# Sparse attention in two groups of four heads, the first woven with a convolution tile and query projections, and a rotation done by transfers

## The chip, the cores and the metric

The kernel runs on one core of one Trainium2 chip. The metric is device time in microseconds (us): the median of three runs, and beside it one execution that was profiled. TensorE (PE) multiplies, VectorE (DVE) and ScalarE (ACT) work on rows of up to 128 partitions, GpSimd (POOL) does small powers and issues some transfers, SyncE (SP) issues most transfers. Transfers may also be issued from the ACT queue.

## The reference

Two layers in float32 on 512 positions of width 1024. The change touches the mixing step of the second layer, where eight heads of a sparse attention stand beside a causal convolution:

```python
def partial_rope(x, cos, sin):                 # the first 16 of each 64 channels are rotated
    x1, x2 = xr[..., :8], xr[..., 8:16]
    rot = jnp.concatenate([x1 * cos - x2 * sin, x2 * cos + x1 * sin], axis=-1)
    return jnp.concatenate([rot.astype(x.dtype), x[..., 16:]], axis=-1)

def dsa_attention(q, k, v, qi, ki, wi):        # for each block of 128 queries
    rel = jax.nn.relu(jnp.einsum('bqhd,bsd->bqhs', qib, ki))
    score = jnp.einsum('bqh,bqhs->bqs', wib, rel)           # index scores, 4 heads
    _, sel = lax.top_k(where(causal, score, -inf), 128)     # 128 keys are kept for each query
    logits = einsum(qb, k[sel]) * (64 ** -0.5)              # 8 heads, one key and value head
    p = softmax(where(sel <= t, logits, -inf)); return einsum(p, v[sel])

q, k, v, qi, ki, wi, glu = jnp.split(rmsnorm(x) @ w_in, cuts, axis=-1)
u = causal_dwconv(ga * sigmoid(gg), conv_b_w, conv_b_b)     # 31 taps, 512 channels
b_out = jax.nn.silu(layernorm(u))
x = x + jnp.concatenate([a_out, b_out], axis=-1) @ w_out
```

## The kernel before

Activations lie transposed (channels on partitions, 512 positions along the free dimension), in pairs of a rounded part (hi) and a remainder (lo). A projection is eight times three matmuls (lines 385 to 387: hi*hi, lo*hi, hi*lo) of 128 channels by 512 positions, so 24 for one output tile. Its weights come by an SP transfer into `raw`, are cast to `whi` on ACT (L361), and the remainder `wlo` is taken on DVE in two halves (L364).

`mix_2` is the stage that changes. It has these parts, in this order:

- `sparse_in` turns the projections `qi` (two tiles) and `ki` into rotated tiles by `roped_2`, and computes the index scores (L1518, six matmuls for a pair of heads and a block of queries), ReLU on ACT (L1486) and the weighted sum `acc` on DVE (L1489, L1491).
- `top_rounds` finds the mask: for each of the query blocks 1, 2 and 3, sixteen rounds of a MAX8 (L1575) and a MATCH_REPLACE8 (L1576) over 256, 384 or 512 keys, all on DVE, each round on the result of the one ahead of it. L1578 ends a block and makes `acc` an additive mask. This chain is woven (`jobs.weave`) with a queue of jobs that mostly need PE: the four pairs of convolution inputs (`conv_in`, 48 matmuls each), three convolution tiles (`conv`, L1695), the key and value projection (`sparse_kv`), the query projections (`sparse_q`, two times 48), and the last convolution tile.
- `sparse_attend` does the attention in 16 steps (a block of queries, a pair of heads): `scores` (six matmuls L1518, on DVE the mask and the row maximum L1604, on ACT the exponential L1606), one step later `turn` (transposes L1616, copied to SBUF L1618), one step later `values` (L1629). At the last pair of a block the sums are inverted, turned (L1638) and multiplied in. It is woven with `conv_out` (layer norm of the convolution), whose transposes are L1732 and L1747. PE runs this part in the order in which the code is written (`manual_schedule`); everywhere else a scheduler orders the instructions of each engine.

`roped_2` rotates one tile. It copies the projection to `x` on ACT (L1527), swaps rows 0 to 7 with rows 8 to 15 of each 64 by a matmul with a constant permutation (L1529), forms x*C2 (L1530), swapped*S2 (L1532) and their sum (L1533) on DVE, and splits the sum in hi on ACT (L409) and lo on DVE (L410). Rows 16 and up have S2 = 0. It is called eight times: twice for `qi`, once for `ki`, once for the key, four times for the queries. `x` and the result `t` come from a ring `t2` of three buffers that also holds `rel`, `dex` and `don`. For `ki` and the key, `both_halves` then copies 64 rows onto the other 64 by two SP transfers (L1510).

The first layer has a similar swap by transfers already (`swap`, L1501: transfers of 32 rows, issued on the ACT queue).

Of the kernel before, what the change touches and what calls it, by code (L numbers as in the profile page):

```python
# [30 lines left out]
NT = 4  # L31
# [8 lines left out]
def _constants():  # L40
# [17 lines left out]
    put("perm2", (i == np.where(m < 8, p + 8, np.where(m < 16, p - 8, -1))[None, :]))  # L58
# [175 lines left out]
FILL = 32  # L234


class Builder:
# [1283 lines left out]
    def roped_2(self, p, dst, ps, n, rows=None):  # L1521
# [58 lines left out]
    def sparse_attend(self, p, tbs, acc, qT, kv, mix):  # L1580
# [5 lines left out]
        R = [p.tile([128, 4, 540], F32, name="ds", tag="R", bufs=2), p.tile([128, 4, 512], F32, name="dPT")]  # L1586
        ring = lambda k, n: R[k][:, n % 4, :512]
        turns = [0, 0]

        def slot(k):  # L1590
            turns[k] += 1
            return ring(k, turns[k])

        def scores(tb, h0):
            n = (tb + 1) * 128
            msk = acc[tb][:, :n] if tb else self.c("swm")[:, 128:256]
            if h0 == 0:
                S["st", tb] = p.tile([128, 4, 8], F32, name="dst", tag="dst", bufs=2)
            st = S["st", tb]
            pss = [self.psum(t) for t in ("at", "mm")]  # L1600
            self.scores_pair(pss, qT[h0 // 2], kT, tb)
            for h, ps in zip((h0, h0 + 1), pss):
                s = S[tb, h] = slot(0)
# [4 lines left out]
            return 0.00334 * n  # L1608

        def turn(tb, h0):  # L1610
            n = (tb + 1) * 128
            for h in (h0, h0 + 1):
                pt = self.psum("rw")
                s = S.pop((tb, h))
                for c in range(tb + 1):
                    tr(pt[:, c * 128:(c + 1) * 128], s[:, c * 128:(c + 1) * 128], self.ident)  # L1616
                PT = S["PT", tb, h] = slot(1)
                (V.tensor_copy if h % 2 else nc.scalar.copy)(PT[:, :n], pt[:, :n])  # L1618
            return 0.22 * (tb + 1)

        def values(tb, h0):

            if h0 == 0:
                S["po"] = self.psum("po")
            po, st, j = S["po"], S["st", tb], h0 // 2
# [5 lines left out]
            if h0 < 6:  # L1631
                return 0.42 * (tb + 1)
            V.reciprocal(st[:, 3], st[:, 2])
            ex = p.tile([128, 512], F32, name="dex", tag="t2", bufs=self.t2n)
# [329 lines left out]
```

## Time and profile before

| | |
|---|---|
| median of three runs | 1451.52 us (1449.52 to 1459.29) |
| profiled execution, its own time | 1450.54 us |
| its span | 1448.8 us |
| PE busy, mean granted clock | 97% of the span, 0.988 |
| DVE, ACT, POOL busy | 60%, 39%, 6% |
| `mix_2` with the end of the norm ahead of it, 728 to 909.8 us | 181.8 us, granted clock 0.94 |

A row of the stretches gives the time of each stretch, the time in which each engine worked in it, and the granted clock of TensorE (1.00 is 2.4 GHz, 0.50 is 1.2 GHz). Idle time of an engine counts where another engine waits for it.

### The profile page before, as it was taken

The page shows a single profiled execution, that of the slowest core. Times are in us where ns is not written, and L with a number is a line of the kernel's source. Part 1 is how long each engine was busy: PE and PEld are TensorE (multiplying, and loading weights), DVE is VectorE, ACT ScalarE, POOL GpSimd, SP SyncE. Part 2 cuts the span into 40 slices and gives each one's busy share as a digit, 9 for nine tenths or more (in the row PEclk, how much of TensorE's full clock was granted, in tenths as well). Part 3 has the DMA queues.
Part 4 walks back from the last instruction along what each step waited for, and adds up shares of the span by engine and source line. Part 5 has one row for each costly group of instructions (what it writes and reads, how often), then busy time and mean ns, then how long its engine had stood idle before and what let it go on. Part 6 is the DMA issues. An engine that isn't in the chain of part 4 may idle for free.

```text
span 1448.8 us, 20320 instructions
## 1 busy us (share of the span) xinstructions
PE 1407.9 (97%) x7876; PEld 1113.7 (77%) x7876; DVE 870.5 (60%) x1983; ACT 557.9 (39%) x964; POOL 89.7 (6%) x164
## 2 busy tenths in 40 slices
PE   8799999999999999999999999999999999999998
PEld 6688768876776887887867556888888888888886
DVE  4768567776756775347569957465465555554232
ACT  4534345444344322333432126443344334343122
POOL 1101011201001000000001100000000000000000
PEclk9999999999999999999999998999999999999999
DMA  8367314422222441325226510252122332332221
GB/s 277 119 187 224 106 39 122 122 61 81 74 73 67 138 131 60 123 69 187 66 66 158 133 59 1 74 190 87 59 88 88 106 99 88 105 99 102 102 87 73
DMA packets 143617, 151.65 MB, mean 105 GB/s; under 512 B 22305, under 2 KB 118945, under 8 KB 143009
## 3 DMA queue, kind: packets, MB, share of 16 engines
q1 hardware_dynamic: 129088, 124.93, 27.6%
q0 software_dynamic: 4480, 14.98, 3.8%
q10 hardware_dynamic: 9952, 10.45, 2.2%
q8 instruction: 62, 1.02, 0.3%
q14 instruction: 35, 0.28, 0.1%
HBM read 135.33 MB, written 13.18 MB: 103 GB/s over the span
## 4 chain that ended last, share of the span: by engine, by line
PE 77%; DVE 8%; issue 2%; ACT 1%; POOL 1%; DMA 1%; ACTq 0%; POOLq 0%; DVEq 0%; SPq 0%
PE ps_mm L385 17%; PE ps_mm L386 17%; PE ps_mm L387 16%; DVE acc L1576 2%; PE ps_at L385 2%; PE ps_rw L385 2%; PE ps_at L387 2%; PE ps_at L386 2%; PE ps_rw L387 2%; PE ps_rw L386 2%; DVE m L1575 2%; DVE wlo L364 1%; PE ps_po L643 1%; PE ps_at L1518 1%; PE ps_at L614 1%
## 5 line engine op out<-in xcount | busy, mean ns | idle before, releaser
L364 DVE TENSOR_TENSOR wlo<-raw,whi 128x512 fp32r<-128x512 f32 x412 | 272.7, 683 | 279.4 <-ACT whi L361 276.1
L361 ACT CAST whi<-raw 128x1024 fp32r<-128x1024 f32 (+1 forms) x206 | 215.9, 1049 | 454.1 <-PE ps_mm L386 247.6
L386 PE MATMUL ps_mm<-blo,whi 128*128 128x512 f32 (+2 forms) x544 | 208.9, 384 | 0.0
L385 PE MATMUL ps_mm<-bhi,whi 128*128 128x512 f32 (+2 forms) x544 | 208.3, 383 | 0.0
L387 PE MATMUL ps_mm<-bhi,wlo 128*128 128x512 f32 (+2 forms) x544 | 207.6, 382 | 0.0
L385 PE MATMUL ps_mm<-hhi,whi 128*128 128x512 f32 (+1 forms) x488 | 195.2, 400 | 0.2 <-ACT hhi L409 0.2
L386 PE MATMUL ps_mm<-hlo,whi 128*128 128x512 f32 (+1 forms) x488 | 192.4, 394 | 0.8 <-DVE hlo L410 0.8
L387 PE MATMUL ps_mm<-hhi,wlo 128*128 128x512 f32 (+1 forms) x488 | 192.4, 394 | 0.0
L386 PEld LDWEIGHTS ps_mm<-blo,whi 128*128 128x128 f32 (+1 forms) x544 | 102.1, 188 | 22.9 <-issue 3.3
L385 PEld LDWEIGHTS ps_mm<-bhi,whi 128*128 128x128 f32 (+1 forms) x544 | 102.0, 188 | 21.5 <-issue 1.8
L387 PEld LDWEIGHTS ps_mm<-bhi,wlo 128*128 128x128 f32 (+1 forms) x544 | 102.0, 188 | 21.4 <-issue 1.8
L385 PEld LDWEIGHTS ps_mm<-hhi,whi 128*128 128x128 f32 x488 | 92.7, 190 | 20.4 <-issue 3.4
L387 PEld LDWEIGHTS ps_mm<-hhi,wlo 128*128 128x128 f32 x488 | 92.8, 190 | 18.2 <-issue 1.8
L386 PEld LDWEIGHTS ps_mm<-hlo,whi 128*128 128x128 f32 x488 | 92.7, 190 | 17.7 <-DVE hlo L410 1.3
L995 DVE TENSOR_TENSOR tmp<-U,L 32x31 f32<-32x31 f32 (+30 forms) x124 | 37.9, 306 | 4.2 <-DMA L<-lspill 2.0
L385 PE MATMUL ps_mm<-yhi,whi 128*128 128x512 f32 x96 | 39.1, 409 | 0.5 <-DVE ga L1183 0.3
L997 DVE TENSOR_TENSOR U<-U,tmp 32x31 f32<-32x31 f32 (+30 forms) x124 | 38.0, 306 | 2.3
L386 PE MATMUL ps_mm<-ylo,whi 128*128 128x512 f32 x96 | 38.7, 404 | 0.0
L387 PE MATMUL ps_mm<-yhi,wlo 128*128 128x512 f32 x96 | 38.3, 399 | 0.0
L421 ACT ACTIVATE nxs<-x 128x1024 f32<-128x1024 f32 x16 | 17.0, 1060 | 32.3 <-DVE x L1210 28.7
L1695 PE MATMUL ps_yk<-R,diag 128*32 128x512 f32 x256 | 29.3, 594 | 0.0
L385 PE MATMUL ps_mm<-mT,whi 128*128 128x256 f32 x96 | 28.0, 291 | 0.7 <-DVE kvt L410 0.6
(478 smaller groups left out, 2629.4 us busy)
## 6 DMA issues: line engine op xcount, KB each, us to landing
raw<-in_w_in_dram SPq DMA_DIRECT2D x24, 1024.0 KB, 5.3
raw<-in_w_in_dram SPq DMA_DIRECT2D x26, 512.0 KB, 3.9
raw<-in_w_gate_dram SPq DMA_DIRECT2D x11, 1024.0 KB, 5.1
raw<-in_w_up_dram SPq DMA_DIRECT2D x11, 1024.0 KB, 5.1
raw<-in_w_down_dram SPq DMA_DIRECT2D x10, 1024.0 KB, 4.9
raw<-in_w_out_dram SPq DMA_DIRECT2D x8, 1024.0 KB, 4.9
R<-cspill POOLq DMA_DIRECT2D x16, 270.0 KB, 6.0
raw<-in_w_k_cross_dram SPq DMA_DIRECT2D x4, 1024.0 KB, 7.8
```

What stands on the lines that cost most here:

```text
L361: nc.scalar.copy(h, v)
L364: self.last_lo = nc.vector.tensor_tensor(l[:, x], v[:, x], h[:, x].bitcast(F32), op=OP.subtract)
L385: mm(ps, L[0], R[0], start=first, stop=False)
L386: mm(ps, L[0], R[1], start=False, stop=False)
L387: mm(ps, L[1], R[0], start=False, stop=last)
L421: nc.scalar.activation(sc, x, AF.Square, accum_out=ss[:, 0:1])
L614: mm(pv[r][:, :n], q[64 * r:64 * r + 64, tb * 128:(tb + 1) * 128], kT[64 * r:64 * r + 64, key0:key0 + n], start=True, stop=True)
L995: V.tensor_tensor(t, U32[:np_, 0:a, m:m + 1].to_broadcast([np_, a, w]), L32[m // 16][:np_, m % 16:m % 16 + 1, m + 1:32].to_broadcast([np_, ...
L997: V.tensor_tensor(U32[:np_, 0:a, m + 1:32], U32[:np_, 0:a, m + 1:32], t, op=OP.add)
L1575: V.max(m, acc[tb][:, :n])
L1576: V.match_replace(acc[tb][:, :n], m, acc[tb][:, :n], DEAD)
L1695: nc.tensor.matmul(ps[32 * b:32 * b + 32], diag(i)[:, b * 8 + g, :], R[:, b, 4 * g:4 * g + 512], start=g == 0, stop=g == 7)
```

## The change

The rotation: the matmul with the permutation goes. Instead the rows of `x` are moved to `t` by transfers on the ACT queue, three for each 64 rows (8 rows, 8 rows, and 48 rows that are copied in place so that `t` is defined), so six for a tile of 128 rows. The product with S2 is then taken in place from `t`. A constant column block goes, and a filler in SBUF grows by as much, which keeps addresses.

The attention: it runs as two groups `g` of four heads. Within a group the blocks of queries are paired as (0, 3) and (1, 2), and steps alternate between the two blocks of a pair; one normalisation serves both blocks of a pair. Group 0 uses two buffers "at" for its scores and is woven with the last convolution tile and the second pair of query projections. Group 1 uses "at" and "mm" and has nothing written between its steps. `conv_out` follows it in the code and is left to the scheduler.

```diff
@@ roped_2
         nc.scalar.copy(x[:rows], ps[:rows])
-        pp = self.psum("at")
-        nc.tensor.matmul(pp[:n], self.c("perm2")[:n, :n], x[:n], start=True, stop=True)
+        t = p.tile([128, 512], F32, name="ry2", tag="t2", bufs=self.t2n)
+        for h in range(0, n, 64):
+            for d, r, k in ((0, 8, 8), (8, 0, 8), (16, 16, 48)):
+                nc.scalar.dma_start(t[h + d:h + d + k], x[h + r:h + r + k])
+        V.tensor_tensor(t[:n], t[:n], S2[:n], op=OP.mult)
         V.tensor_tensor(x[:n], x[:n], C2[:n], op=OP.mult)
-        t = p.tile([128, 512], F32, name="ry2", tag="t2", bufs=self.t2n)
-        V.tensor_tensor(t[:n], pp[:n], S2[:n], op=OP.mult)
         V.tensor_tensor(t[:n], x[:n], t[:n], op=OP.add)
@@ sparse_attend
-        steps = [(tb, h) for tb in tbs for h in range(0, 8, 2)]
-        for i in range(len(steps) + 2):
+        steps = [(G, i, h0) for G in ((0, 3), (1, 2)) for h0 in (0, 2) for i in range(2)]
+        for n in range(len(steps) + 2):
             for k, f in enumerate((scores, turn, values)):
-                if 0 <= i - k < len(steps):
-                    yield f(*steps[i - k])
+                if 0 <= n - k < len(steps):
+                    f(*steps[n - k])
+            yield fill
@@ mix_2
-        jobs.add(ci[0], dj[0], ci[1], dj[1], co[0], dj[2], ci[2], co[1], dj[3], ci[3], co[2], self.sparse_kv(p, hT, kv),
-                 self.sparse_q(p, hT, 0, qT), co[3], self.sparse_q(p, hT, 1, qT))
+        jobs.add(ci[0], dj[0], ci[1], dj[1], co[0], dj[2], ci[2], co[1], dj[3], ci[3],
+                 self.sparse_kv(p, hT, kv), self.sparse_q(p, hT, 0, qT), co[2])
         jobs.weave(self.top_rounds(p, acc), self.SC2[0])
+        jobs.run(lambda: not jobs.q)
+        tail = Jobs()
+        tail.add(co[3], self.sparse_q(p, hT, 1, qT))
+        tail.load(tail.q[1])
         jobs.run()
+        jobs = tail
         mix = self.act_tiles("h")
-        jobs.add((None, lambda _: self.sparse_attend(p, range(NT), acc, qT, kv, mix)))
+        self.rings, self.turns = [], [0, 0]
+        attend = lambda g, tags, fill: self.sparse_attend(p, g, acc, qT, kv, mix, tags, fill)
         with self.tc.manual_schedule(engines={mybir.EngineType.PE}):
-            jobs.weave(self.conv_out(p, cv, mix), self.SC2[1])
+            jobs.weave(attend(0, ("at", "at"), 1.0), self.SC2[1])
             jobs.run()
+            for _ in attend(1, ("at", "mm"), 0.0):
+                pass
+        for _ in self.conv_out(p, cv, mix):
+            pass
         return mix
-    SC2 = (1.3, 18.0)
+    SC2 = (1.3, 1.9)
```

Three places show the new order. The first is ACT at the rotations of `sparse_in` (`rx` is x, `ry` is t, `hl` a rotated tile). Before:

```order
L1527 COPY rx_6584<-ps_mm 128x512
L361 CAST whi<-raw 128x1024
L1527 COPY rx_6596<-ps_mm 128x512
L409 CAST hl<-ry_6589 128x512
L409 CAST hl<-ry_6601 128x512
L361 CAST whi<-raw 128x1024
L1527 COPY rx_6640<-ps_mm 68x512
L409 CAST hl<-ry_6645 64x512
```

and now, with the lines of the changed kernel:

```order
L1526 COPY rx_6600<-ps_mm 128x512
L360 CAST whi<-raw 128x1024 x2
L408 CAST hl<-ry_6586 128x512
L1530 DMA ry_6602<-rx_6600 8x512 x2
L1530 DMA ry_6602<-rx_6600 48x512
L1530 DMA ry_6602<-rx_6600 8x512 x2
L1530 DMA ry_6602<-rx_6600 48x512
L1526 COPY rx_6648<-ps_mm 68x512
L360 CAST whi<-raw 128x1024
L1679 ACTIVATE sth<-ps_mm 128x512
L408 CAST hl<-ry_6602 128x512
L1530 DMA ry_6650<-rx_6648 8x512 x2
```

The transfers of the second tile stand behind the cast of the first rotated tile, and those of `ki` behind the cast of the second.

The second is DVE at the end of the rounds. Before, L1578 of block 3 stands right behind the last round and all of the key's and queries' rotation behind it:

```order
L1575 MAX m_7275<-acc 128x8
L1576 MATCH_REPLACE acc<-m_7275,acc 128x512
L1578 TENSOR_SCALAR acc<-acc 128x512
L1530 TENSOR_TENSOR rx_7348<-rx_7348,rp_6109 64x512
L1532 TENSOR_TENSOR ry_7353<-ps_at,rp_6109 64x512
```

Now the rotations of the key and of one query tile stand among the rounds, and of the next query tile its first product does:

```order
L1575 MAX m_7295<-acc 128x8
L1576 MATCH_REPLACE acc<-m_7295,acc 128x512
L1531 TENSOR_TENSOR ry_7412<-ry_7412,rp_6109 128x512
L1578 TENSOR_SCALAR acc<-acc 128x512
L1532 TENSOR_TENSOR rx_7410<-rx_7410,rp_6109 128x512
L1608 ISA ds,dst<-ps_at,acc 128x512
```

The third is PE where the attention begins (`ps_yk<-R,diag` is the convolution). Before, after the last rotation:

```order
L1732 MATMUL ps_yk<-cst,cv 128x128 x4
L1529 MATMUL ps_at<-rx_7551,cst 128x512
L1518 MATMUL ps_at<-hl 128x256
L1518 MATMUL ps_mm<-hl 128x256
L1518 MATMUL ps_at<-hl 128x256
```

and now:

```order
L1703 MATMUL ps_yk<-R,diag 32x512 x32
L1517 MATMUL ps_at<-hl 128x256 x6
L1703 MATMUL ps_yk<-R,diag 32x512 x12
L1517 MATMUL ps_at<-hl 128x512 x6
L1620 MATMUL ps_rw<-cst,ds 128x128 x2
L1703 MATMUL ps_yk<-R,diag 32x512 x8
L1517 MATMUL ps_at<-hl 128x256 x6
```

Blocks 0 and 3 now come first, with pieces of the last convolution tile between them. From the first rotation to the first index score PE has 24 projection matmuls for `ki` and then 20 others before, 79 others now; from the last index score to the first attention score it has 166 projection matmuls and three convolution tiles now. Outside `mix_2` every engine has the same instructions in the same order.

## Rows read from the trace of the kernel before

**Rows 1.** The page's head and busy times of the engines over the whole span.

```profile
span 1448.8 us, 20320 instructions
PE 1407.9 (97%) x7876; PEld 1113.7 (77%) x7876; DVE 870.5 (60%) x1983; ACT 557.9 (39%) x964; POOL 89.7 (6%) x164
```

**Rows 2.** Stretches of `mix_2`: time, busy time of each engine, granted clock (PEclk), share of the transfer engines, GB/s. The last row is the whole.

```profile
728.00:745.60 17.60, 17.60 (x90) 12.18 (x88) 10.17 (x17) 5.50 (x8) 0.00 (x0) 1.00 0.31 81
745.60:753.50 7.90, 7.62 (x34) 4.64 (x33) 3.63 (x8) 3.54 (x8) 0.00 (x0) 1.00 0.39 100
753.50:827.30 73.80, 73.80 (x423) 46.86 (x423) 71.61 (x178) 15.72 (x22) 11.04 (x20) 1.00 0.54 140
827.30:861.80 34.50, 30.86 (x151) 17.81 (x151) 17.88 (x31) 9.19 (x13) 0.00 (x0) 0.95 0.21 69
861.80:882.80 21.00, 18.63 (x108) 11.99 (x106) 13.39 (x67) 11.43 (x41) 0.99 (x2) 0.59 0.00 1
882.80:909.80 27.00, 25.71 (x241) 18.16 (x239) 21.92 (x74) 19.93 (x52) 1.81 (x4) 1.00 0.06 20
728.00:909.80 181.80, 174.21 (x1037) 111.64 (x1037) 138.59 (x370) 65.31 (x141) 13.84 (x25) 0.94 0.31 85
```

**Rows 3.** What PE waited for from 728 to 910 us: total us, times, longest (the three largest).

```profile
PE ps_at L1529 <- ACT rx L1527: 3.6, 2, 2.7
PE ps_rw L1616 <- ACT ds L1606: 2.3, 4, 1.3
PE ps_at L1518 <- DVE lnst L1736: 0.8, 1, 0.8
```

**Rows 4.** PE in order of time (start, us, what): a rotation by matmul and what follows it, a row of projections, a convolution tile.

```profile
741.11 1.07 PE L1529 MATMUL ps_at<-rx,cst 64*64 64x512 f32 x2
742.11 0.40 PE L1468 MATMUL ps_at<-cst,rx 4*128 4x4 f32 x4
...
745.63 0.38 PE L1518 MATMUL ps_at<-hl 64*128 64x256 f32 x1
...
780.10 0.39 PE L385 MATMUL ps_mm<-bhi,whi 128*128 128x512 f32 x1
780.32 0.39 PE L386 MATMUL ps_mm<-blo,whi 128*128 128x512 f32 x1
780.64 7.07 PE L1695 MATMUL ps_yk<-R,diag 128*32 128x512 f32 x64
```

**Rows 5.** PE in order of time where the granted clock falls, with the idle time ahead of an instruction in brackets, and the same form of work at either clock (868 and 883 us).

```profile
831.62 2.07 PE L1529 MATMUL ps_at<-rx,cst 128*128 128x512 f32 x2 [2.69 <-ACT rx L1527]
834.63 0.40 PE L386 MATMUL ps_mm<-blo,whi 128*128 128x512 f32 x1
...
864.96 0.33 PE L1616 MATMUL ps_rw<-cst,ds 128*128 128x128 f32 x1 [1.29 <-ACT ds L1606]
...
868.86 0.69 PE L1616 MATMUL ps_rw<-cst,ds 128*128 128x128 f32 x2
...
883.61 0.66 PE L1616 MATMUL ps_rw<-cst,ds 128*128 128x128 f32 x4
```

**Rows 6.** DVE in order of time: the first MAX8, the last round and the end of block 3.

```profile
753.51 0.42 DVE L1575 MAX8 m<-acc 128x8 f32<-128x256 f32 x1
...
825.42 0.69 DVE L1575 MAX8 m<-acc 128x8 f32<-128x512 f32 x1
...
826.23 0.67 DVE L1576 MATCH_REPLACE8 acc<-m,acc 128x512 f32<-128x512 f32 x1
826.94 0.43 DVE L1578 TENSOR_SCALAR acc<-acc 128x512 f32<-128x512 f32 x1
```

**Rows 7.** The first layer's swap by transfers (32 rows, 64 KB each, ACT queue): duration of an issue min/median/max in ns, three issues in a row, and the longest way from issue to landing with the instruction that waited for it.

```profile
L1501 ACTq DMA_DIRECT2D ry<-rx x20: 514/602/626, 217.0 to 289.5; - x20
DMA to landing us min/median/max: 2.0/3.5/5.5
...
277.65 1.82 ACTq L1501 DMA_DIRECT2D ry<-rx  x3
...
284.50 0.69 DVE L546 TENSOR_TENSOR rx<-ry,tabs 128x512 f32<-128x512 f32 x1 [1.09 <-DMA ry<-rx]
```

**Rows 8.** The copy of 64 rows in `mix_2` (`both_halves`, SP queue), and the share of the transfer engines (next to last column) in two stretches at the first rotations and in one at the swap of rows 7.

```profile
DMA to landing us min/median/max: 2.2/2.2/2.2
...
729.00:736.00 7.00, 7.00 (x42) 5.15 (x41) 2.83 (x5) 2.42 (x4) 0.00 (x0) 1.00 0.02 6
736.00:742.00 6.00, 6.00 (x25) 3.35 (x23) 4.65 (x8) 2.46 (x4) 0.00 (x0) 1.00 0.35 87
277.00:285.00 8.00, 8.00 (x47) 6.93 (x46) 3.37 (x10) 2.70 (x4) 1.64 (x1) 1.00 0.90 229
```

**Rows 9.** ACT and DVE in order of time at the first rotation: the copy, DVE's products and sum, the cast.

```profile
729.55 0.59 ACT L1527 COPY rx<-ps_mm 128x512 f32<-128x512 f32 x1 [4.05 <-PE ps_mm L387]
733.78 0.68 DVE L1532 TENSOR_TENSOR ry<-ps_at,rp 128x512 f32<-128x512 f32 x1
734.38 0.68 DVE L364 TENSOR_TENSOR wlo<-raw,whi 128x512 fp32r<-128x512 f32 x1
734.98 0.68 DVE L1533 TENSOR_TENSOR ry<-rx,ry 128x512 f32<-128x512 f32 x1
735.70 0.62 ACT L409 CAST hl<-ry 128x512 fp32r<-128x512 f32 x1 [1.93 <-DVE ry L1533]
```

More of the change, by code (lines that the diff above doesn't have):

```diff
@@ L232 @@
 PASS = 0.64
-FILL = 32
+FILL = 160
 class Builder:
@@ L1585, in sparse_attend, with scores @@
         S = {}
-        R = [p.tile([128, 4, 540], F32, name="ds", tag="R", bufs=2), p.tile([128, 4, 512], F32, name="dPT")]
-        ring = lambda k, n: R[k][:, n % 4, :512]
-        turns = [0, 0]
+        if not self.rings:
+            self.rings = [p.tile([128, 4, 540], F32, name="ds", tag="R", bufs=2), p.tile([128, 4, 512], F32, name="dPT")]
+        R = self.rings
+        turns = self.turns
         def slot(k):
             turns[k] += 1
-            return ring(k, turns[k])
-        def scores(tb, h0):
+            return R[k][:, turns[k] % 4, :512]
+        def scores(G, i, h0):
+            tb = G[i]
             n = (tb + 1) * 128
             msk = acc[tb][:, :n] if tb else self.c("swm")[:, 128:256]
[L1597 to L1603, printed above, removed]
+            if (i, h0) == (0, 0):
+                S["st", G] = p.tile([128, 4, 8], F32, name="dst", tag="dst", bufs=2)
+            st = S["st", G]
+            pss = [self.psum(t) for t in tags]
+            self.scores_pair(pss, qT[2 * g + h0 // 2], kT, tb)
+            for r, ps in enumerate(pss):
+                h = 4 * i + h0 + r
+                s = S[tb, h0 + r] = slot(0)
                 V.tensor_tensor_reduce(s[:, :n], ps[:, :n], msk, 1.0, DEAD, OP.add, OP.max, st[:, 0, h:h + 1])
@@ L1607, in scores, with turn, values @@
                                      accum_out=st[:, 2, h:h + 1])
-            return 0.00334 * n
-        def turn(tb, h0):
+        def turn(G, i, h0):
+            tb = G[i]
             n = (tb + 1) * 128
-            for h in (h0, h0 + 1):
+            for r in range(2):
                 pt = self.psum("rw")
-                s = S.pop((tb, h))
+                s = S.pop((tb, h0 + r))
                 for c in range(tb + 1):
                     tr(pt[:, c * 128:(c + 1) * 128], s[:, c * 128:(c + 1) * 128], self.ident)
[L1617 to L1623, printed above, removed]
-                S["po"] = self.psum("po")
-            po, st, j = S["po"], S["st", tb], h0 // 2
+                PT = S["PT", tb, h0 + r] = slot(1)
+                (V.tensor_copy if r else nc.scalar.copy)(PT[:, :n], pt[:, :n])
+            if (i, h0) == (1, 2):
+                st = S["st", G]
+                V.reciprocal(st[:, 3], st[:, 2])
+                ex = S["ex"] = p.tile([128, 512], F32, name="dex", tag="t2", bufs=self.t2n)
+                nc.scalar.copy(ex.rearrange("p (h d) -> p h d", h=8), st[:, 3, :, None].to_broadcast([128, 8, 64]))
+        def values(G, i, h0):
+            tb = G[i]
+            if (i, h0) == (0, 0):
+                S["po"] = self.psum("po")
+            po = S["po"]
+            last = (i, h0) == (1, 2)
+            if last:
+                ex, rb = S.pop("ex"), self.psum("rw")
+                for j in range(4):
+                    tr(rb[:, j * 128:(j + 1) * 128], ex[:, j * 128:(j + 1) * 128], self.ident)
+                nc.scalar.copy(ex, rb)
+            j = 2 * i + h0 // 2
             PT = [S.pop(("PT", tb, h0 + r)) for r in range(2)]
```

24 lines of the change are left out of this document (7 added, 17 removed).

## The prediction

> **What bounds the kernel now.** First the page: TensorE is busy for 97% of the span, at a granted clock that is full nearly everywhere [rows 1]. So a gain must come from matmuls that vanish, from idle time of TensorE, or from time at the lower clock. The change is confined to one stage, 728 to 909.8 us; the stretches show where it loses [rows 2]. TensorE works 174.2 of 181.8 us, so 7.6 us are idle, and its clock is 0.94. Nearly all of that lies in two stretches: 827.3 to 861.8 (0.95, 3.6 us idle) and 861.8 to 882.8 (0.59, 2.4 us idle). In time at the lower level of 1.2 GHz this costs at most 0.05 x 34.5 + 0.41 x 21.0 = 10.3 us. The waits name what TensorE waited for: 3.6 us for the copy ahead of a rotation (2.69 us of it once), 2.3 us for exponentials [rows 3]. In order of time the clock drops after the wait of 2.69 us and is back some 3 us later in dense projections (834.63, 0.40 us); it drops again after waits near 865 us and stays low for 17 us of small matmuls, where two transposes take 0.69 us and later four take 0.66 us [rows 5].
>
> The second bound is DVE. From the first MAX8 at 753.51 to the end of block 3 at 826.94 [rows 6] it works 71.6 of 73.8 us [rows 2], while TensorE is full with jobs that don't need its result. The attention needs the mask. Today it starts at 861.8, long after the rounds, so their length is hidden. That is the cover to watch.
>
> **What is saved.** Eight rotations by matmul go. One occupies TensorE from 741.11 to 742.11 [rows 4], so 8 x 1.0 = 8.0 us. Idle time and clock are worth at most 7.6 + 10.3 us. If all were won, the stage would be 25.9 us shorter.
>
> **What the rotation costs now.** A tile of 128 rows needs six transfers. An issue on the ACT queue takes 0.60 us, and landing took 2.0 to 5.5 us, 3.5 in the middle, for the first layer's similar swap [rows 7]. The slow ones fell where the transfer engines were 0.90 busy; here they are 0.02 and 0.35 busy, and the copy of 64 rows in this stage lands in 2.2 us [rows 8]. I take 2.3 us and keep 2.0 and 5.5 as ends. The Trainium skill (DMA: Bandwidth & Descriptors, Bandwidth) asks for transfers of 1 MiB and calls those under 64 KB dominated by their descriptors, which speaks against pieces of 8 rows. The same page (Anatomy of one DMA) gives some 2.0 us fixed per transfer; by it each rotation would be about 0.3 us shorter than by my sum, and the swap's middle of 3.5 us doesn't agree with it.
>
> The ring of three buffers makes the first three rotations serial: the target of the second is the source of the first, free when DVE has summed it, and ACT's order says the same. From the copy (729.55 + 0.59 [rows 9]):
>
> - First: five issues of 0.6 ahead of the last, 2.3 us landing: 735.4. Then four DVE steps (two products, a sum, a weight split) at 0.6 us apart [rows 9]: 737.9.
> - Second, by the same steps, 3.0 + 2.3 + 2.4: 745.6.
> - Third, for the index key, three transfers and three DVE steps, 1.2 + 2.3 + 1.8: 750.9. Cast 0.6 and the copy to the other half 2.2: 753.7.
>
> TensorE reaches the first index scores after 59 more projection matmuls than before, at 0.225 us each [rows 4], less three rotations: 745.6 + 13.3 - 3.0 = 755.9. So TensorE's own order sets this point, and the rotation is hidden with 2 us to spare.
>
> **The rounds end later.** Before, 7.9 us passed from the first index score to the first MAX8 [rows 4, 6]. Two weight splits (1.2 us) no longer stand there, so the rounds begin at 755.9 + 6.7 = 762.6. They took 73.4 us; now DVE also has among them nine rotation steps (9 x 0.6), a copy, two short score reductions and one split more, about 7.2 us. The end of block 3 moves from 826.94 to 762.6 + 80.6 = 843.2. Then come a product, two masked reductions of 512 and a sum, some 3.5 us, before TensorE can go on with the third score pair: 846.7.
>
> **TensorE comes early.** Its index scores took 12.6 us with the same 19 projections between them (I take that over): 768.5. Then 166 projections (37.4 us), three convolution tiles (3 x 7.0 [rows 4]) and four transposes (0.4): 827.3. Two score pairs, 20 of 32 pieces of the last convolution tile and two transposes are 6.5 us: 833.8. From there it is idle until 846.7: **12.9 us**, a wait on the mask that takes the place of the old ones.
>
> **The rest.** TensorE's work in the stage at full clock is 174.2 - 10.3 - 8.0 = 155.9 us. By 833.8, without an idle moment, 105.8 are done; 50.1 are left, so 896.8. Group 0 is woven with 13.5 us of dense work, and I take no wait in it. Group 1 begins right behind the last query projection, whose rotation it needs at its third step: copy 0.6, five issues 3.0, landing 2.3, three products and sums 1.9, cast and remainder 1.2, makes 9.0 us, against some 4 us of work that stands between: 5 us idle. Inside group 1 I keep 1.5 us of the old waits for exponentials. For the clock I take 1.4 us after the first stall (half of some 3 us at 1.2 GHz, [rows 5]) and for group 1 a third of the 8.6 us which 861.8 to 882.8 cost [rows 2], since it is half of the attention and DVE sets part of its pace: 2.9 us. Sum: 896.8 + 5 + 1.5 + 1.4 + 2.9 = 907.6 against 909.8, so 2.2 us less. ACT's 42 issues (25 us of its queue) lie in a stage where it works 65 of 182 us [rows 2]; I cost them at nothing. If they held up the casts of weights, the projections would wait. Constants and filler cost nothing.
>
> On the profiled execution's 1450.5 us this is 1448.3. The median of the three runs is 1 us above that execution, so I expect **1449 us**. About 1% (14.5 us) is what a measurement of this kernel can tell from no change.
>
> **Rivals.**
>
> - *The gain of the weave mostly arrives.* The last query tile's rotation is covered by the convolution's transposes, which the scheduler may put in that gap, and group 1 stays at full clock. Then 5, 1.5 and 2.9 us fall away: 898.2, about 1439.5 us. For it: at full clock the larger half of the attention ran 27 us with 1.3 us idle [rows 2]. Against it: the drop at 865 us came after waits of about a microsecond [rows 5]. If also the wait on the mask were shorter by 4 us, it would be 1435.5.
> - *Slower: the serial rotations land late.* At 5.5 us, the far end of rows 7, each is 3.2 us longer. Three in series lose 9.6 us, of which 2 are slack, so the rounds and the mask are 7.6 us later; the last one adds 3.2. That is 10.8 us on the forecast, 1460 us, 8.6 slower than before. It decides from a landing of 3.4 us on, where 4 x 1.05 less the slack of 2 is the forecast gain of 2.2. For it: weights and convolution rows move at the same time (0.54 over the rounds [rows 2]), and the swap at 0.90 took longest. Against it: 0.02 to 0.35 at the first rotations and 2.2 us for the neighbouring copy [rows 8]. The Trainium skill (Trainium Kernel Development and Optimization, Key Constraints) says that transfers of all queues share the same 16 engines and interleave, which this rival would need.
> - *The clock falls and stays down.* After the stall of 12.9 us both groups run at 1.2 GHz as 861.8 to 882.8 did. Twice 8.6 us in place of 4.3 taken: 1462 us. Against it: group 0 has dense projections, and in dense projections the clock came back after 3 us.
>
> **The numbers.** Forecast 0.54, the gain arriving 0.22, late rotations 0.14, low clock 0.06; 0.04 is left for others. The range of 1436 to 1461 us holds the first three and leaves out part of the low clock and a gain beyond 13 us. Faster by over 1% (under 1437) needs most of the first rival and more: 0.12. Slower by over 1% (over 1466) needs late rotations together with the low clock: 0.07. Within 1%: 0.81.
>
> **What would show it.** Index scores beginning near 756 us, not 746; the last L1578 near 843 us; DVE full between; one wait of TensorE of some 13 us for the mask near 834 to 847 us, and one of about 5 us at the first step of group 1 that needs the last query tile; landings near 2.3 us on the ACT queue; projections at full clock from 850 to 875 us; end of the attention near 907 us. I am wrong if the rounds end before 838 us (then faster), if landings are over 3.4 us (then slower), or if weight casts on ACT stand behind transfers and the projections ahead of the attention show waits.

## The result and the profile after

The changed kernel takes 1472.71 us (median of four runs, 1470.80 to 1475.49), the kernel before 1451.95 us beside it: ratio 1.0132, 95% interval 1.0102 to 1.0162. It is 20.8 us slower; 1449 us was forecast.

The head of the page, against [rows 1]:

```profile
span 1473.7 us, 20358 instructions
PE 1410.6 (96%) x7860; PEld 1117.8 (76%) x7860; DVE 870.1 (59%) x1983; ACT 557.4 (38%) x964; POOL 89.7 (6%) x164
```

I measure the stage from its first copy for a rotation to the start of the last group of value matmuls. Before, that was 729.55 to 909.08, 179.5 us; now it is 737.19 to 936.75, 199.6 us. These 20.0 us are about the difference of the medians. (That last group is 32 matmuls in the old order and 12 in the new one, so what follows the stage is not quite the same either: 539.7 us before, 537.0 us now.) The stretches answer to [rows 2], with the same columns; the first row is the stage, begun 1.55 us ahead of the copy as there.

```profile
735.64:936.80 201.16, 175.09 (x1040) 113.57 (x1039) 138.28 (x370) 64.99 (x141) 13.83 (x25) 0.89 0.33 86
735.64:764.60 28.96, 28.26 (x143) 22.36 (x141) 13.29 (x22) 9.13 (x13) 2.81 (x5) 1.00 0.44 121
764.60:785.70 21.10, 17.27 (x57) 10.12 (x57) 9.65 (x25) 5.81 (x13) 0.00 (x0) 0.70 0.39 86
785.70:846.00 60.30, 60.30 (x362) 37.28 (x362) 55.35 (x139) 11.26 (x15) 8.22 (x15) 0.99 0.54 138
846.00:854.50 8.50, 0.01 (x2) 0.00 (x0) 8.36 (x18) 2.74 (x4) 0.00 (x0) 0.82 0.47 152
854.50:902.20 47.70, 43.94 (x297) 25.90 (x297) 30.66 (x95) 18.93 (x51) 1.10 (x2) 0.89 0.11 34
902.20:936.80 34.60, 25.31 (x185) 17.90 (x185) 20.96 (x75) 17.13 (x48) 1.70 (x3) 0.75 0.08 24
```

TensorE is idle for 26.1 us in place of 7.6. Its busy time has not fallen (175.1 against 174.2 us) although the eight rotations of some 1.0 us are gone: the granted clock is 0.89 in place of 0.94. Four places lose: the index scores (764.6 to 785.7, 3.8 us idle, clock 0.70), a gap ahead of group 0 (8.5 us), and both groups. The five largest waits of TensorE in the stage, against [rows 3], show for what (total us, times, longest):

```profile
PE ps_at L1517 <- ACT hl L408: 12.1, 3, 8.5
PE ps_yk L1740 <- DVE yn L1734: 4.8, 1, 4.8
PE ps_at L1517 <- DMA hl<-hl: 3.7, 1, 3.7
PE ps_yk L1740 <- DVE dst L1625: 2.2, 1, 2.2
PE ps_at L1517 <- DVE hl L409: 0.9, 1, 0.9
```

`hl` is a rotated tile, cast by ACT at the end of its rotation. ACT in order of time (ACTq are its issues of transfers): the three rotations ahead of the index scores, the key and the first query tile ahead of group 0, the last query tile in group 1.

```profile
737.19 0.59 ACT L1526 COPY rx<-ps_mm 128x512 f32<-128x512 f32 x1 [3.83 <-PE ps_mm L386]
737.81 4.51 ACTq L1530 DMA_DIRECT2D ry<-rx  x6
742.36 0.59 ACT L1526 COPY rx<-ps_mm 128x512 f32<-128x512 f32 x1 [4.58 <-issue]
...
747.06 3.80 ACTq L1530 DMA_DIRECT2D ry<-rx  x6
...
756.75 1.90 ACTq L1530 DMA_DIRECT2D ry<-rx  x3
...
828.93 1.94 ACTq L1530 DMA_DIRECT2D ry<-rx  x3
...
834.34 0.58 ACT L1526 COPY rx<-ps_mm 128x512 f32<-128x512 f32 x1
842.28 0.62 ACT L408 CAST hl<-ry 64x512 fp32r<-64x512 f32 x1 [7.36 <-DVE ry L1533]
842.28 3.91 ACTq L1530 DMA_DIRECT2D ry<-rx  x6
...
853.87 0.62 ACT L408 CAST hl<-ry 128x512 fp32r<-128x512 f32 x1 [5.46 <-DVE ry L1533]
...
903.63 3.87 ACTq L1530 DMA_DIRECT2D ry<-rx  x6
907.55 0.40 ACT L1610 ACTIVATE ds<-ds,dst 128x128 f32<-128x128 f32 x1 [3.43 <-DMA ry<-rx]
```

The second tile is copied at 742.36, but its transfers go out at 747.06, when DVE has summed the first tile and a buffer of the ring is free. The first query tile is copied at 834.34; its transfers stand on ACT behind the key's cast until 842.28, and the buffer that they write is free no sooner, as e3 will show. That cast waits for DVE, and DVE for the key's transfers, as the chain of waits has it (start, us):

```profile
828.93 0.68 ACTq L1530
829.65 0.63 ACTq L1530
830.32 8.66 DMA ry<-rx
839.10 0.68 DVE ry L1531
```

In these 8.66 us the convolution's rows (four transfers of 270 KB) and a megabyte of weights were under way. The index part has a slow landing too: the copy of the index key's second half took 6.91 us, where [rows 8] had 2.2; four transfers of the convolution's rows were under way beside it as well. The first index tile had landed in 2.29 us; the second was waited for until 754.21, 3.3 us behind the end of its last issue. The rows are from the chain of waits, from DVE, and from the stretches (the share of the transfer engines is the next to last number):

```profile
741.76 2.29 DMA ry<-rx
...
764.56 6.91 DMA hl<-hl
```

```profile
754.21 0.69 DVE L1531 TENSOR_TENSOR ry<-ry,rp 128x512 f32<-128x512 f32 x1 [0.99 <-DMA ry<-rx]
```

```profile
737.80:744.10 6.30, 6.30 (x37) 4.58 (x36) 0.18 (x1) 1.53 (x2) 0.00 (x0) 1.00 0.16 42
764.50:771.50 7.00, 3.42 (x13) 2.01 (x12) 1.79 (x4) 0.90 (x3) 0.00 (x0) 1.00 1.04 219
830.30:839.00 8.70, 8.70 (x43) 6.93 (x45) 5.66 (x13) 1.54 (x2) 0.53 (x1) 1.00 1.00 253
```

TensorE at the same places:

```profile
764.62 0.38 PE L1517 MATMUL ps_at<-hl 64*128 64x256 f32 x1
...
771.60 0.62 PE L1517 MATMUL ps_at<-hl 64*128 64x256 f32 x4 [3.68 <-DMA hl<-hl]
...
838.94 7.07 PE L1703 MATMUL ps_yk<-R,diag 128*32 128x512 f32 x64
854.54 0.87 PE L1517 MATMUL ps_at<-hl 64*128 64x256 f32 x4 [8.53 <-ACT hl L408]
...
909.35 0.66 PE L1740 MATMUL ps_yk<-cst,cv 128*128 128x128 f32 x2 [4.83 <-DVE yn L1734]
...
914.27 0.58 PE L1517 MATMUL ps_at<-hl 64*128 64x256 f32 x1 [3.40 <-ACT hl L408]
```

### The profile page after: what moved, and what is told of

Read it like the earlier page. It is cut to its first block, busy times and chain, and to the rows that moved or that the text cites. A ratio compares the mean times of both kernels' runs of the same rounds, so it can differ in the third digit from the quotient of the medians.

```text
span 1473.7 us, 20358 instructions
## 1 busy us (share of the span) xinstructions
PE 1410.6 (96%) x7860; PEld 1117.8 (76%) x7860; DVE 870.1 (59%) x1983; ACT 557.4 (38%) x964; POOL 89.7 (6%) x164
## 4 chain that ended last, share of the span: by engine, by line
PE 44%; DVE 2%; DMA 1%; issue 1%; ACT 1%; ACTq 1%; POOL 0%; POOLq 0%; DVEq 0%
PE ps_mm L384 9%; PE ps_mm L385 9%; PE ps_mm L386 9%; PE ps_yk L1703 1%; PE ps_at L384 1%; PE ps_rw L384 1%; PE ps_at L385 1%; PE ps_at L386 1%; PE ps_rw L386 1%; PE ps_rw L385 1%; PE ps_at L1517 1%; PE ps_po L1645 1%; DMA ry<-rx 1%; PE ps_rw L1620 1%; PE ps_yk L386 1%
## 5 line engine op out<-in xcount | busy, mean ns | idle before, releaser
L385 PEld LDWEIGHTS ps_mm<-hlo,whi 128*128 128x128 f32 x488 | 92.5, 190 | 17.6 <-DVE hlo L409 1.2
L1517 PE MATMUL ps_at<-hl 64*128 64x256 f32 (+2 forms) x108 | 24.3, 445 | 17.2 <-ACT hl L408 12.1
L386 PE MATMUL ps_mm<-yhi,wlo 128*128 128x512 f32 x96 | 38.3, 399 | 0.0
L1517 PEld LDWEIGHTS ps_at<-hl 64*128 64x128 f32 x108 | 14.2, 231 | 29.8 <-ACT hl L408 14.7
```

The costliest lines, as they stand in the source:

```text
L385: mm(ps, L[0], R[1], start=False, stop=False)
L386: mm(ps, L[1], R[0], start=False, stop=last)
L1517: self.nc.tensor.matmul(pss[r][:, :n], q[a][c, tb * 128:(tb + 1) * 128], k[b][c, :n], start=i == 0, stop=i == 2)
```

## The experiments

All runs in one table. "Stage" is the measure above, from one profiled execution of each run; those of e1 and f1 were 5 us faster than the medians of these runs. The ratio is to the kernel before on the same chip, with its 95% interval. The kernel before had medians from 1451.95 to 1455.09 us there, so between rows the ratios compare better than the medians.

| run | stage us | median us | ratio |
|---|---|---|---|
| before | 179.5 | 1451.95 | 1 |
| the change | 199.6 | 1472.71 | 1.0132 (1.0102 to 1.0162) |
| e1: all eight rotations by matmul | 179.0 | 1455.36 | 1.0011 (0.9983 to 1.0040) |
| e2: kernel before, rotations by transfers | 186.8 | 1463.35 | 1.0076 (1.0052 to 1.0100) |
| e3: transfers issued by POOL | 190.1 | 1469.78 | 1.0116 (1.0087 to 1.0144) |
| e4: end of the convolution woven into group 1 | 200.1 | 1472.31 | 1.0133 (1.0102 to 1.0164) |
| e5: index rotations by matmul | 189.0 | 1460.44 | 1.0034 (1.0011 to 1.0056) |
| e6: only index rotations by transfers | 187.2 | 1462.06 | 1.0040 (1.0015 to 1.0064) |
| e7: the key's rotation by matmul | 200.1 | 1470.54 | 1.0101 (1.0066 to 1.0136) |
| e8: first two query tiles earlier | 199.5 | 1475.10 | 1.0130 (1.0088 to 1.0173) |
| f1: only last two query tiles by transfers | 185.5 | 1460.49 | 1.0035 (1.0012 to 1.0057) |
| f2: four transfers per tile | 194.6 | 1468.08 | 1.0106 (1.0039 to 1.0173) |
| f3: index targets out of the ring | 185.9 | 1461.32 | 1.0053 (1.0028 to 1.0079) |
| f4: index transfers issued by POOL | 186.6 | 1467.01 | 1.0087 (1.0059 to 1.0116) |
| g2: f3, key and queries by matmul | 177.1 | 1450.82 | 0.9967 (0.9941 to 0.9994) |
| g4: g2, projections ahead of the convolution tile | 177.5 | 1451.20 | 0.9969 (0.9939 to 1.0000) |
| g3: g4, last two query tiles by transfers | 171.7 | 1451.46 | 0.9973 (0.9949 to 0.9997) |
| g1: seven rotations by transfers, covered | 173.1 | 1449.81 | 0.9962 (0.9942 to 0.9982) |

**Which half of the change costs the time?** e1 takes the transfers out and leaves the rest; e2 puts them into the kernel before.

```diff
-        for h in range(0, n, 64):
-            for d, r, k in ((0, 8, 8), (8, 0, 8), (16, 16, 48)):
-                nc.scalar.dma_start(t[h + d:h + d + k], x[h + r:h + r + k])
-        V.tensor_tensor(t[:n], t[:n], S2[:n], op=OP.mult)
+        pp = self.psum("at")
+        nc.tensor.matmul(pp[:n], self.c("perm2")[:n, :n], x[:n], start=True, stop=True)
...
+        V.tensor_tensor(t[:n], pp[:n], S2[:n], op=OP.mult)
```

> The changed kernel with the rotation by the permutation matmul again (eight matmuls of about 1.0 us, no transfers); the new grouping, the weave and the order of the jobs stay. Theory R (the transfers cost the time: index scores 27.4 us after the first copy in place of 16.1, then 3.7 us on the key's second half, then 9.5 us on the first query tile and 3.4 us on the last one, with the clock at 1.2 GHz after each stall): the first index score comes back to 16 to 19 us after the first copy, no wait above 3 us ahead of group 0 that names a rotation, and the time falls to 1448 to 1456 us. Theory O (the order costs it: the key, the value and the first queries now stand last before the attention, and the transposes of the convolution's end wait inside group 1): the first index score comes back too, but the waits at group 0 (now on the mask) and in group 1 stay, and the time is 1462 to 1470 us.

> The kernel before with the rotation by transfers and nothing else changed. Theory R: the first index scores come 10 to 12 us later and the last rotation ahead of the attention takes some 9 us in place of 3.6 us of waiting, with more time at 1.2 GHz, against 8 us of matmuls saved: 1456 to 1466 us. Theory O: in the old order the rotations are covered, except for the index key, so the saved matmuls and the wait cancel: 1448 to 1455 us.

e1 is back at the time of before: in the new order the transfers make the whole loss, and the new grouping by itself gives nothing that can be measured. e2 is 10 us slower than before, and its stage some 7 us longer, against 20.0 in the change: the same transfers lose in the old order too, but half as much or less. The largest waits of TensorE in e1 are of the old kind, and its stretch (columns as above) has the clock at 0.98:

```profile
PE ps_at L1529 <- ACT rx L1527: 5.2, 3, 3.2
PE ps_rw L1620 <- ACT ds L1610: 1.4, 3, 0.9
```

```profile
730.41:910.96 180.55, 172.07 (x1055) 109.80 (x1053) 137.25 (x370) 64.99 (x141) 13.83 (x25) 0.98 0.32 86
```

**Who issues, and the convolution's end.** e3 writes `nc.gpsimd` for `nc.scalar` in the loop of transfers. e4 advances `conv_out` inside group 1:

```diff
+            out = self.conv_out(p, cv, mix)
             for _ in attend(1, ("at", "mm"), 0.0):
-                pass
-        for _ in self.conv_out(p, cv, mix):
+                next(out, None)
+            for _ in out:
                 pass
```

> The changed kernel with the rotation's 42 transfers issued by POOL instead of ACT. If the loss is that ACT's order holds transfers back behind casts (the query tile's six transfers stood from 834.9 to 842.3 us behind the key's cast) and casts behind transfers, the wait of 8.5 us ahead of group 0 falls below 5 us, the first index scores come 2 to 5 us earlier, and the time is 1462 to 1468 us. If it is the transfers' own landing (the key's took until 837.9, 7 us after their issue, while the convolution's rows and a megabyte of weights moved), it stays within 1469 to 1476 us; it gets above 1476 us if POOL's issue is slower than ACT's 0.63 us each.

> The changed kernel with the end of the convolution (its transposes, normalisation and gate) advanced by one step after each step of group 1 inside TensorE's fixed order, as it was woven into the attention before, in place of being left to the scheduler behind it. If the waits of TensorE for its normalisation (4.8 us and 2.2 us) and the low clock behind them (group 1 from 914 to 923 us) cost the time, 6 to 10 us less: 1463 to 1467 us. If the last query tile's rotation holds group 1 at the same point anyway, or the normalisation's chain of some 3.5 us per block waits just as long in the woven order, 1469 to 1476 us.

e3's median is 3 us lower, at the edge of the second range and within the intervals. Its stage is 9.5 us shorter; of this 3.6 us come back behind it (540.6 us to the end in place of 537.0). The last group of index scores begins 38.3 us after the first copy in place of 46.7, but the wait ahead of group 0 grows:

```profile
850.74 1.31 PE L1517 MATMUL ps_at<-hl 64*128 64x256 f32 x6 [14.67 <-ACT hl L408]
```

POOL's issues show why. The key's go out behind the convolution's rows, 5.6 us after its copy at 817.69. The first query tile is copied by 830.5, and no cast stands on this queue; yet POOL stands idle, 18.04 us in all, until DVE has summed the key, which frees a buffer of the ring:

```profile
821.14 2.18 POOL L1688 DMA_DIRECT2D R<-cspill  x4 [3.06 <-DMA cspill<-u]
823.30 1.58 POOL L1530 DMA_DIRECT2D ry<-rx  x3
842.92 3.10 POOL L1530 DMA_DIRECT2D ry<-rx  x6 [18.04 <-DVE ry L1533]
```

So ahead of group 0 the ring holds the query tile as well as ACT's order does; no run frees it there.

e4 changes neither the stage nor the median, though the waits at the convolution's transposes nearly go. What follows its stage is 3.2 us shorter (533.8 us), as the convolution's end is done by then; the medians do not show it. In e4 the exponentials (`ds`) and the rotated tile show in their place:

```profile
902.13 0.33 PE L1620 MATMUL ps_rw<-cst,ds 128*128 128x128 f32 x1 [3.71 <-ACT ds L1610]
906.54 0.58 PE L1517 MATMUL ps_at<-hl 64*128 64x256 f32 x1 [3.48 <-ACT hl L408]
```

So the waits of 4.8 and 2.2 us lay in the shadow of the last query tile's rotation, whose six issues also hold back ACT's exponentials, by 3.43 us at 907.55 above.

**Which rotations?** e5 does the three index rotations by matmul, e6 the five others, e7 the key's alone, f1 all but the last two; e8 moves the first two query tiles.

```diff
+        if mat:
+            pp = self.psum("at")
...
# e8
-        jobs.add(ci[0], dj[0], ci[1], dj[1], co[0], dj[2], ci[2], co[1], dj[3], ci[3],
-                 self.sparse_kv(p, hT, kv), self.sparse_q(p, hT, 0, qT), co[2])
+        jobs.add(ci[0], dj[0], ci[1], dj[1], co[0], self.sparse_q(p, hT, 0, qT), dj[2], ci[2], co[1], dj[3], ci[3],
+                 self.sparse_kv(p, hT, kv), co[2])
```

> The changed kernel with the three rotations ahead of the index scores by the permutation matmul, the five others by transfers. All eight by matmul gave 1455.4 us, all by transfers 1472.7, so 17.3 us are to be divided. If the late index scores are the larger part (11 us later, the wait of 3.7 us for the key's second half, 13.7 us at 1.2 GHz, and through the rounds all that follows), 1457 to 1463 us. If the chain key, first queries, group 0 is (8.5 + 0.9 us of waiting, 10.2 us at 1.2 GHz behind it, then the last query tile), 1465 to 1470 us, with that wait still above 8 us.

> The mirror of the run before: only the three rotations ahead of the index scores by transfers, the key's and the four query tiles' by matmul. Index part the larger: 1464 to 1470 us, with a wait for the mask (about 5 to 10 us) in place of the wait for the rotated query tile. Chain ahead of group 0 the larger: 1457 to 1463 us. If the parts are independent, the losses of the two runs against 1455.4 us add up to 17 us; if one covers the other, they add up to less.

> The changed kernel with one rotation of eight by matmul: that of the attention's key, whose three transfers took until 837.9 us and held, through ACT's order, the first query tile's six until 842.3 us, and through DVE's order the rounds for 3.0 us. If that queue of one behind the other makes the wait of 8.5 us ahead of group 0, that wait falls to 0 to 4 us and the time to 1464 to 1468 us. If each tile's transfers are late by themselves, the wait stays above 6 us and the time at 1470 to 1474 us.

> The changed kernel with its first two query tiles projected and rotated by transfers some 60 us earlier, behind the first convolution tile instead of behind the key; only the key and the last convolution tile but one stand between there and group 0. If cover by dense work is what the transfers lacked, the two tiles cost nothing there, the wait ahead of group 0 is for the key alone (its transfers, landing behind the convolution's rows) and 3 to 6 us shorter: 1464 to 1469 us. If the key alone makes the wait, no change: 1470 to 1475 us, and with the queries gone from behind it less work covers it, so the wait may even grow.

> The changed kernel with only the last two query tiles (woven with group 0, needed by group 1) rotated by transfers, the six others by matmul. From the first copy of the stage to the last values it took 179.0 us with all eight by matmul and 189.0 with the key's and all four query tiles' by transfers. If group 1's waits (4.8 us at the convolution's transposes, 3.4 us for the rotated tile, then 1.2 GHz) are the larger share of these 10 us, 184 to 188 us here and 1459 to 1463 us in all. If the key and the first query tiles ahead of group 0 are, 180 to 183 us here and 1454 to 1458 us.

Against e1 the stage of e5 is 10.0 us longer, of e6 8.2, of f1 6.5. So the index rotations and the five others cost about as much; of the latter, the last two query tiles cost 6.5 us, which leaves 3.5 for the key with the first two. In the stage the parts make 18.2 of 20.6 us; by the ratios only 3.3 and 4.2 of 17.6 us, with intervals of some 3.5 us for each run, so whether they add fully stays open. e7 and e8 missed: e7 halves the wait ahead of group 0 (4.25 us) and e8 lowers it to 6.62, and neither gets faster by more than the intervals, as the next late thing takes over (in e7 the third score pair waits 1.30 us for DVE, in e8 the key's copy is late by 1.71 and 0.82 us) and the index part keeps its cost. Only in e6 does TensorE wait long for the mask, 3.8 us, as the rounds end late there and group 0 comes early.

**Why are the index rotations late?** f2 copies fewer rows (POOL sets the others to zero), f3 takes the targets out of the ring, f4 lets POOL issue these 15 transfers only.

```diff
# f2
+        nc.gpsimd.memset(t[:n], 0.0)
         for h in range(0, n, 64):
-            for d, r, k in ((0, 8, 8), (8, 0, 8), (16, 16, 48)):
+            for d, r, k in ((0, 8, 8), (8, 0, 8)):
# f3
+        rr = p.tile([128, 4, 540], F32, name="rr", tag="R", bufs=2)
-            self.roped_2(p, qiT[a], ps, 128)
+            self.roped_2(p, qiT[a], ps, 128, t=rr[:, a, :512])
```

> The changed kernel with four transfers per tile of 128 rows in place of six (two for the key tiles): the 48 rows that the sine table multiplies by zero are set to zero by POOL and not copied. 42 issues become 28. If the number of issues on ACT, 0.63 us each, sets the length of each rotation, the first index score comes 2.5 to 4 us sooner than 27.4 us after the first copy, and the time is 1465 to 1469 us. If it is the fixed time of a landing and the order of the queues, under 1.5 us sooner and 1470 to 1475 us.

> The changed kernel with the targets of the first three rotations' transfers in a tile of their own, in place of the ring of three buffers: the second tile's transfers no longer wait until DVE has summed the first. If the ring makes these rotations serial, as the prediction has it, the second tile's six issues start near 743 us of that trace in place of 747, the first index score comes 4 to 7 us sooner than 27.4 us after the copy, and the time is 1463 to 1468 us. If ACT's own order does it (issues, casts that wait for a sum, weight casts that wait for TensorE), it stays above 25 us and the time at 1469 to 1475 us.

> The changed kernel with the transfers of the first three rotations issued by POOL, the others by ACT. With all of them on POOL the time was 1469.8 us: the index scores ended 38.3 us after the first copy in place of 46.7, with the full clock, but the wait ahead of group 0 grew to 14.7 us, as the key's transfers stood behind the convolution's rows on POOL. If these two cancelled, this kernel has the gain alone: 190 to 193 us from the first copy to the last values, 1460 to 1466 us. If a later start of DVE's rounds gives the gain back, 1468 to 1473 us.

f3 wins 13.7 us in the stage and 11 us in the median. ACT in f3 issues the second tile's transfers right behind its copy:

```profile
741.91 0.59 ACT L1527 COPY rx<-ps_mm 128x512 f32<-128x512 f32 x1 [4.57 <-issue]
742.40 1.05 ACT L360 CAST whi<-raw 128x1024 fp32r<-128x1024 f32 x1
742.53 3.27 ACTq L1532 DMA_DIRECT2D rr<-rx  x5
```

The first index score comes 21.9 us after the first copy (27.4 in the change, 16.1 before), the last group of them begins at 34.6 (46.7); TensorE's wait for the key's second half is gone, and the clock does not fall there. The number of issues is a smaller part: f2 brings the first score forward by 2.1 us; its median is 4.6 us lower, which its interval cannot tell from nothing.

f4 leaves the ring as it is, and its stage is 13.0 us shorter all the same. POOL still waits for DVE's sums:

```profile
749.19 3.10 POOL L1530 DMA_DIRECT2D ry<-rx  x6 [4.32 <-DVE ry L1533]
759.78 1.57 POOL L1530 DMA_DIRECT2D ry<-rx  x3 [7.50 <-DVE ry L1533]
```

The first index score comes at 25.6 us, only 1.9 sooner. But TensorE then waits at most 0.8 us for the key's second half, and the clock stays full through the index scores, as in f3 (f3's stretch, then f4's, against 0.70 in the change):

```profile
758.60:772.50 13.90, 13.62 (x62) 8.61 (x62) 8.37 (x20) 5.87 (x13) 2.49 (x5) 1.00 0.90 222
766.40:781.00 14.60, 13.33 (x60) 8.32 (x60) 9.13 (x25) 6.22 (x14) 1.47 (x3) 1.00 0.58 134
```

So a serial chain need not cost this much: what costs is the stall at the key's second half with the low clock behind it, and either run avoids it. (f2 keeps a stall of 3.3 us there, and a clock of 0.68 through its index scores.) The Trainium skill (DMA: Bandwidth & Descriptors, Issuing engines are not separate DMA queues) says that issuing from several engines only saves the time of issuing. An issue takes POOL 0.53 us (median in e3) and ACT 0.63, so for 15 issues that would be 1.5 us; the 13.0 us of the stage are more, by the stall that did not come. f4's median fell less than its stage, by 5.7 us; why stays open. Its profiled execution began the stage late, at 740.85 us.

**Do transfers cost anything where they are covered?** g2 is f3 with the key and the queries by matmul. g4 weaves the last projections ahead of the last convolution tile, g3 then rotates these two tiles by transfers, g1 also the first two, in the order of e8; the key stays with the matmul.

```diff
# g3, g4, g1
-        tail.add(co[3], self.sparse_q(p, hT, 1, qT))
-        tail.load(tail.q[1])
+        tail.add(self.sparse_q(p, hT, 1, qT), co[3])
+        tail.load(tail.q[0])
```

> The changed kernel with the three index rotations by transfers into a tile of their own, the key and the four query tiles by matmul. If transfers cost nothing where they have a buffer, the stage is the 179.0 us of eight matmuls less up to 3 us of TensorE: 176 to 179 us, and 1450 to 1455 us. If they keep a cost (the first index score still came 21.9 us after the first copy in place of 16.1), 181 to 185 us, and 1457 to 1462 us.

> As the run with the tile of its own and the rest by matmul, but the last two query tiles by transfers as well, and their projections woven ahead of the last convolution tile instead of behind it, so that 7 us of convolution and several steps of group 0 stand between the transfers and group 1. If cover was what lacked, the 6.5 us that the two tiles cost at the end do not come: 174 to 178 us for the stage, 1448 to 1454 us. If they cost it wherever they stand, 181 to 186 us, 1456 to 1462 us.

> The order of the last run (query projections ahead of the last convolution tile) with these two tiles by matmul. If the order has an effect of its own, this differs from the run with the tile of its own and the rest by matmul by 2 us or more; if not, both agree within 2 us, and the difference to the last run is what two rotations by transfers cost or save (up to 2 us saved).

> Seven of eight rotations by transfers, each where it has cover: the index three into a tile of their own, the first two query tiles behind the first convolution tile, the last two ahead of the last convolution tile; the key, which has no cover, by matmul. If transfers are free where they are covered: 172 to 177 us for the stage and 1446 to 1452 us, the fastest of all. If the waits only move (DVE's rotation steps behind the rounds, the ring again for the query tiles, since the score tiles of the index use it too), 180 to 188 us and 1456 to 1464 us.

They do not. The stage of g2 is 1.9 us shorter than that of e1 with three matmuls less, though its first index score still comes 5.8 us later. g3 differs from g4 by two rotations alone and has the shortest stage of all, 171.7 us in place of 177.5, and the full clock throughout; TensorE's waits for the copies ahead of a matmul rotation fall from 5.6 to 2.3 us with them:

```profile
737.26:910.51 173.25, 164.54 (x1035) 105.57 (x1033) 134.90 (x366) 64.16 (x141) 13.29 (x24) 1.00 0.36 96
```

All four are as fast as the kernel before or slightly faster; between them the medians cannot decide. In g1, g3 and g4 some 2 us of the shorter stage come back behind it (539.1 to 539.4 us to the end, 537.4 in g2). g1, with seven rotations by transfers, has the lowest median: 0.9962 of before with an interval wholly under 1, like those of g2 and g3, and 1.6% under the change.

**How much belongs to the stage?** Both kernels were profiled once more, unchanged.

> The kernel before, unchanged, profiled once more. If the begin of the stage scatters with the clock of the first layer from execution to execution, its first copy lies anywhere from 729 to 741 us, 2 us or more from 729.55, while the stage keeps its length of 180.2 us within 1 us. If the begin belongs to the kernel, it is 729.6 within 0.5 us again.

> The changed kernel, unchanged, profiled once more. Scatter: first copy 2 us or more away from 737.19 us, stage 199.6 us within 1.5 us. Belonging to the kernel: 737.2 within 0.5 us again.

The stage kept its length: 178.9 us (179.5) for the kernel before, 200.1 (199.6) for the changed one. Its begin moved from 729.55 to 734.17 us for the kernel before; for the changed one it was 737.48 after 737.19. So 4.6 of the 7.6 us between the two first profiles need no effect of the change.

## Why the prediction was wrong, by its steps

- **The saving** of 8.0 us for eight rotations and at most 17.9 for idle time and clock was there in part: g3, with five rotations by transfers, the full clock and still 8.7 us idle, has a stage 7.8 us shorter than before. What failed is what stood against it.
- **"The rotation is hidden with 2 us to spare."** Wrong. The first index score was forecast 26.4 us after the first copy and came at 27.4, so that point was nearly right. But the key's second half, forecast 24.2 us after the copy, landed at 34.3: the serial rotations up to the key's cast took 27.4 us in place of 22.0, and the copy behind them 6.91 in place of 2.2. So the slack of 2 us was overrun, and the index scores, for which I took over 12.6 us, took some 21: TensorE waited 3.68 us and the clock fell to 0.70. Without this stall the stage was 13.7 (f3) or 13.0 us shorter (f4).
- **The rounds** began 40.3 us after the copy (forecast 33.1) and block 3 ended after 125.2 (forecast 113.7). The late begin is the index scores' again. Between the two it is 84.8 us for 80.6; f3 has 32.9 and 110.7, so the count of DVE's steps was good. What I left out there is that DVE stands still in order behind the key's transfers, for 3.04 us at 839.10.
- **The wait of 12.9 us for the mask** until 117.2 us after the copy: TensorE did wait until 117.4, by accident. It waited for the rotated first query tile, 8.5 us, and came itself later than forecast. The rotations of the key and the first query tiles do not stand in my sum, and I gave no reason: from the key's copy to the first scores it is 26.2 us, of which 8.66 are the key's transfers, and the projections and the convolution tile behind the copy covered 17.7 of them.
- **"ACT's 42 issues: I cost them at nothing."** Wrong: they hold back exponentials (3.43 us at 907.55) and stand behind casts themselves (834.34 to 842.28, where the ring holds them too). The text's warning was of weight casts and projections; it was the rotations and the exponentials.
- **Group 0 without a wait, 5 us in group 1, 4.3 us for the clock.** Group 0's stretch has 3.8 us idle at 0.89, group 1's 9.3 us idle at 0.75. f1 prices the last two tiles at 6.5 us, near the 5 us taken. The clock was the larger error: by the prediction's own way of counting (the part of the clock that is lacking, times the length of each stretch in which TensorE works) the rows above give some 21 us where 4.3 were taken; idle time is 26.1 us where 12.9 + 5 + 1.5 = 19.4 were taken.
- **The rivals.** Late, serial rotations (1460 us, chance 0.14) was the right mechanism at half its size. It was to decide from a landing of 3.4 us. The first index tile landed in 2.29 us, as taken; the second took more than 3 us, and the copy of the index key's second half (6.91 us) and the attention's key (8.66 us) lay above my far end of 5.5 from [rows 7]. The low clock (1462 us) came along with it, behind the stalls. I had given these two chances one by one, though one brings the other about. The weave's gain (1439.5 us) needed cover that the change does not give.

The Trainium skill (DMA: Bandwidth & Descriptors, Anatomy of one DMA) gives some 2.0 us fixed per transfer, for transfers that GpSimd issues. The first rotation, issued by ACT, is near it with 2.29 us; beside the convolution's rows the key's took 8.66 us, for which that section has no term.

## What to carry to other kernels

Moving work from TensorE to transfers cost nothing here where dense work covered issue, landing and the vector steps behind it (g1, g3), and the index rotations reached that with a buffer of their own; so count, for each moved step, the ring it writes, the queue of the engine that issues it, and what stands behind it there. Price a chain by its slowest landing next to the bulk transfers that run at that moment, not by the middle of quiet ones. And don't add a stall and the low clock as separate risks: where a stall went, as at the index scores in f3 and f4 (1.00 in place of 0.70), the clock came back with it.

## What was not expected of the hardware

- The begin of the stage scatters from execution to execution, over all profiles here from 729.6 to 740.9 us, and by 4.6 us for one and the same kernel; the granted clock over the first 350 us was 0.99 in the first profile of before and 0.96 in f4 and g3. Two profiles are better compared from a mark inside the kernel than by their spans.
- Three small transfers took 2.3 us behind their last issue for the index key (758.65 to 760.98) and 8.2 us for the attention's key (830.87 to 839.10), both on the ACT queue. The transfer engines were 0.68 busy in the first case (756.7 to 760.7 us) and 1.00 in the second; that their load alone makes the difference is not shown.
- POOL issues a transfer in 0.53 us, ACT in 0.63, and one of ACT's took 1.24.
